# The low part of one weight block in a Strassen-like product: from a VectorE subtraction to a ScalarE negation and an adding DMA

## Chip, core and metric

One core of a Trainium2 chip runs the kernel. The metric is the device time of one execution in microseconds; lower is better. The kernel before took 1702.33 us as the median of three runs (1701.73 to 1704.52).

The engines are named as the profile names them: PE (TensorE matmuls; PEld is its weight load), DVE (VectorE), ACT (ScalarE), POOL (GpSimd) and SP (SyncE, which here issues most DMAs). Each engine executes its own list of instructions in order and waits for others through semaphores.

## What is computed

A two-layer encoder trunk runs over two requests (512 and 256 tokens, 768 together) with a width of 1024. Layer 0 mixes tokens by windowed attention, layer 1 by a gated short convolution; each is followed by an MLP and a gated embedding.

```python
for i in range(DEPTH):
    h = rms_norm(x, norm_mix[i])
    if i % N_MIXERS == 0:
        x = x + window_attention(h, attn_w_qkv[j], attn_w_o[j], attn_sink[j], band_bias, in_window)
    else:
        x = x + short_conv(h, conv_w_in[j], conv_w[j], conv_w_out[j])
    h = rms_norm(x, norm_mlp[i])
    x = x + jnp.square(jax.nn.relu(h @ mlp_w_up[i])) @ mlp_w_down[i]
    gate = jax.nn.sigmoid(rms_norm(x, norm_ple[i]) @ ple_w_gate[i])
    x = x + (p[i] @ ple_w_proj[i]) * gate
return rms_norm(x, final_norm)
```

Everything is float32. The MLP is 1024 to 4096 and back.

## The kernel before

**Split numbers.** A matrix product of float32 values is made from operands split in two: a high part, which ACT writes by copying the value to the type fp32r, and a low part, the value minus the high part, which DVE writes. A product is then high x high, high x low and low x high.

**Seven-product pairs.** Most of the large products (the MLP's up and down projections, the convolution's input projection) take two weight chunks at a time as a 2x2 block matrix, w11, w12, w21, w22, each 128x512, and form the 2x2 block product with seven block products instead of eight. `Weights7` holds one such pair: two raw chunks `wraw` of 128x1024 loaded by SP (r1 and r2), two sums of blocks (`sum`), and the split parts of four groups: "direct" (w11 and w12, tiles `whi` and `wlo`), "s32" (tiles `zhi`, `zlo`), "s14" (`whi`, `wlo` again, there are two buffers), and "w22" (the right half of the second chunk, tiles `vhi`, `vlo`, one buffer each). `high(group)` is the ACT copy, `low(group)` the DVE subtraction, `split` both.

**The order in a pair.** PE runs seven products of 12 matmuls each, in the order w11, s3, s2, w12, s1, w22, s4. In each, the matmuls with high weights come first and those with low weights last. The PSUM tile `a` accumulates: after w11 it is copied by ACT (tile `c` in `up` and `seven`, two tiles `C` in `down`), then s2 is added to the same `a`. So s2 may start only when ACT has made the copy. While one pair is multiplied, ACT and DVE prepare the next one: its sums, its "s32" and "direct" groups. Its "s14" group and "w22" are made at the start of its own pair.

**Who uses it.** `up(u)` makes one pair of hidden chunks, `down(g, h)` one pair of output chunks, `seven` one pair of the convolution's input projection. In each MLP the jobs run as: two plain `up`s, then for each of seven groups an even `up`, two `down`s, and an odd `up`. So after the first even `up` the cycle is down, down, up (odd), up (even). There are 28 seven-product pairs in each MLP and 11 in the convolution, 67 in all. After an `up` ACT still squares the result in two steps (line 941): tile y2 first, then y1.

**What sets the order.** Inside these functions the order in which the code calls the engines is the order on PE, ACT and DVE (`manual_schedule`). SP and POOL are ordered by the scheduler; POOL does almost nothing before, and its queue holds no DMA.

## Time and profile before

| | before |
|---|---|
| median of three runs | 1702.33 us |
| the profiled execution | 1702.36 us |
| its span, first to last instruction | 1700.6 us |
| DVE busy | 1415.1 us, 83% |
| ACT busy | 907.5 us, 53% |
| POOL busy | 1.0 us |
| DMA, mean | 85 GB/s |

The profile is of one execution. A row of a timeline has the start in us, the length in us, the engine, the line, the operation with output tile and inputs, and in brackets the idle time of the engine before it with what ended it. A row of waits has who waited for whom, the total in us, how often, and the longest. A PE that is busy all the time bounds the kernel; idle time of other engines costs only what it makes PE wait.

### The profile page before, as it was taken

To read this page: it belongs to the slowest core of one execution; us is meant where nothing else is said; L and a number is where in the kernel's file an instruction comes from. 1 tells how busy PE (TensorE), PEld (TensorE's weight loads), DVE (VectorE), ACT (ScalarE), POOL (GpSimd) and SP (SyncE) were. 2 spreads that over 40 slices of the span, in tenths; PEclk is the share of its full clock that TensorE was granted. 3 is DMA by queue.
4 is the path that set the end of the run, shared out by engine and by line. 5 is a ranking of instruction groups with operands and counts; after the bars stand their busy time and mean duration, and the time that the engine had idled before them with its cause. 6 is when DMAs were issued, how large, how long until landed. Compare 5 with 4: busy or idle time off the path is not lost.

```text
span 1700.6 us, 24086 instructions
## 1 busy us (share of the span) xinstructions
PE 1653.7 (97%) x9410; PEld 1592.2 (94%) x9410; DVE 1415.1 (83%) x2304; ACT 907.5 (53%) x1451; POOL 1.0 (0%) x12
## 2 busy tenths in 40 slices
PE   8999999989999999999999999999999999999996
PEld 7887788989999999999999999999999999999986
DVE  6588888889999989987888877858999999998776
ACT  6367756754455455544654334545445445554544
POOL 0000000000000000000000000000000000000000
PEclk9999999999999999999999999999999999999998
DMA  8654322211122211221212212211122211222222
GB/s 262 193 135 121 106 81 81 87 50 67 71 76 74 74 70 68 74 99 66 100 60 75 74 63 76 76 61 50 62 75 74 74 67 72 75 74 86 82 76 93
DMA packets 47843, 144.58 MB, mean 85 GB/s; under 512 B 6081, under 2 KB 10689, under 8 KB 47729
## 3 DMA queue, kind: packets, MB, share of 16 engines
q1 hardware_dynamic: 45168, 139.89, 24.2%
q10 hardware_dynamic: 2560, 3.15, 0.7%
q8 instruction: 74, 1.21, 0.3%
q14 instruction: 41, 0.33, 0.1%
HBM read 123.10 MB, written 10.48 MB: 79 GB/s over the span
## 4 chain that ended last, share of the span: by engine, by line
PE 59%; DVE 29%; ACT 8%; issue 3%; DMA 0%; DVEq 0%; ACTq 0%; SPq 0%
PE a L466 17%; PE mm L129 9%; PE mm L138 8%; PE b L466 4%; PE gate L138 4%; PE B L466 3%; PE C L466 3%; DVE t L361 3%; DVE wlo L445 3%; DVE y L938 3%; DVE zlo L445 2%; DVE act L394 1%; PE d L466 1%; ACT y L941 1%; DVE sum L410 1%
## 5 line engine op out<-in xcount | busy, mean ns | idle before, releaser
L434 ACT ACTIVATE whi<-sum 128x1024 fp32r<-128x1024 f32 x67 | 70.5, 1052 | 146.9 <-PE a L466 146.9
L941 ACT ACTIVATE y<-y 128x768 f32<-128x768 f32 x64 | 53.7, 840 | 144.6 <-DVE y L938 144.5
L466 PE MATMUL a<-xs,whi 128*128 128x384 f32 x624 | 123.4, 340 | 4.2 <-ACT whi L434 3.4
L466 PEld LDWEIGHTS a<-xs,whi 128*128 128x128 f32 x624 | 111.2, 189 | 4.9 <-ACT whi L434 3.7
L466 PE MATMUL a<-t,zhi 128*128 128x384 f32 x536 | 109.9, 338 | 3.4 <-ACT c L1054 3.1
L466 PE MATMUL b<-t,zhi 128*128 128x384 f32 x536 | 109.4, 338 | 0.5 <-ACT ln L254 0.5
L466 PE MATMUL a<-t,whi 128*128 128x384 f32 x536 | 108.8, 336 | 0.9 <-ACT d L1547 0.9
L466 PEld LDWEIGHTS a<-t,zhi 128*128 128x128 f32 x536 | 94.9, 188 | 4.3 <-ACT c L1054 3.8
L466 PE MATMUL a<-act,whi 128*128 128x384 f32 x448 | 96.5, 337 | 0.0
L466 PEld LDWEIGHTS b<-t,zhi 128*128 128x128 f32 x536 | 95.4, 189 | 0.9 <-ACT ln L254 0.9
L466 PEld LDWEIGHTS a<-t,whi 128*128 128x128 f32 x536 | 94.8, 188 | 1.2 <-ACT d L1547 1.2
L445 DVE TENSOR_TENSOR wlo<-wraw,whi 128x1024 fp32r<-128x1024 f32 x72 | 87.7, 1217 | 6.8 <-ACT whi L434 6.8
L445 DVE TENSOR_TENSOR wlo<-sum,whi 128x1024 fp32r<-128x1024 f32 x67 | 81.9, 1222 | 10.2 <-ACT whi L434 10.2
L1110 DVE TENSOR_TENSOR x<-x,a 128x384 f32<-128x384 f32 x112 | 60.7, 552 | 33.9 <-PE a L466 33.6
L434 ACT ACTIVATE zhi<-sum 128x1024 fp32r<-128x1024 f32 x67 | 71.0, 1060 | 22.3 <-DVE sum L410 22.2
L138 PE MATMUL mm<-xs_mix,whi 128*128 128x512 f32 (+1 forms) x320 | 82.9, 342 | 0.0
L434 ACT ACTIVATE whi<-wraw 128x1024 fp32r<-128x1024 f32 x72 | 75.7, 1052 | 11.6 <-PE C L466 6.1
L445 DVE TENSOR_TENSOR zlo<-sum,zhi 128x1024 fp32r<-128x1024 f32 x67 | 81.6, 1217 | 0.0
L466 PEld LDWEIGHTS a<-act,whi 128*128 128x128 f32 x448 | 79.9, 188 | 0.0
L355 ACT ACTIVATE t<-y 128x768 fp32r<-128x768 f32 x56 | 47.1, 842 | 41.2 <-DVE y L346 30.7
L83 ACT ACTIVATE whi<-wraw 128x1024 fp32r<-128x1024 f32 (+2 forms) x49 | 50.0, 1019 | 34.4 <-PE mm L129 13.9
L466 PE MATMUL a<-xs,wlo 128*128 128x384 f32 x312 | 67.7, 339 | 0.1
(316 smaller groups left out, 4488.0 us busy)
## 6 DMA issues: line engine op xcount, KB each, us to landing
wraw<-in_up SPq DMA_DIRECT2D x64, 512.0 KB, 3.5
wraw<-in_down SPq DMA_DIRECT2D x64, 512.0 KB, 3.5
wraw<-in_w_in SPq DMA_DIRECT2D x24, 512.0 KB, 3.5
wraw<-in_gate SPq DMA_DIRECT2D x16, 512.0 KB, 3.5
pj<-pjs SPq DMA_DIRECT2D x16, 384.0 KB, 3.3
wraw<-in_w_q SPq DMA_DIRECT2D x8, 512.0 KB, 4.8
wraw<-in_w_out SPq DMA_DIRECT2D x8, 512.0 KB, 3.5
x_in<-in_x SPq DMA_DIRECT2D x8, 384.0 KB, 7.6
```

Source lines behind the costliest of these rows:

```text
L83: first = act.activation(hi, src, AF.Copy)
L129: pe.matmul(t, lhsT=w, rhs=x[:, o:e], start=first and i == 0 and j == 0, stop=last and i == n - 1 and j == 2)
L138: pe.matmul(ps[:, o:e], lhsT=w, rhs=x[:, o:e], start=i == 0 and j == 0, stop=i == n - 1 and j == 2,)
L355: act.activation(t[0][:], (self.q1, self.q2)[i][:], AF.Copy)
L361: dve.tensor_tensor(lo[:], (self.q1, self.q2)[i][:], hi[:].bitcast(F32), ALU.subtract)
L394: dve.tensor_tensor(lo[:], self.q2[:], hi[:].bitcast(F32), ALU.subtract)
L434: act.activation(hi[:], src, AF.Copy)
L445: dve.tensor_tensor(lo[:], src, hi[:].bitcast(F32), ALU.subtract)
L466: pe.matmul(ps, lhsT=a, rhs=b, start=start and i == 0, stop=i == len(terms) - 1, skip_group_check=True)
L938: dve.scalar_tensor_tensor(t[:, o:e], src, 0.0, r[:, o:e], op, ALU.mult)
L941: act.activation(t[:], t[:], AF.Square)
L1110: dve.tensor_tensor(t[:, o : o + H], t[:, o : o + H], f, op)
```

## The change

Only the w22 group changes, in all 67 pairs. `high("w22")` now does three things: ACT copies w22 to `vhi` as before; ACT then writes `vlo` as the copy of `vhi` times -1; and POOL issues a DMA that reads w22 once more from HBM and adds it to `vlo` in SBUF, so that `vlo` ends as w22 minus its high part. DVE no longer touches `vlo`. And the call moves: from behind the copy of `a` (in `up`, `down` and `seven`) to the very start of the pair, ahead of the split of "s14".

```diff
             self.raw = [fetch(src1), fetch(src2)]
+            self.src2 = src2
...
             act.activation(hi[:], src, AF.Copy)
+            if tag == "v":
+                self.due.remove(group)
+                act.activation(lo[:], hi[:].bitcast(F32), AF.Copy, scale=-1.0)
+                nc.gpsimd.dma_start(lo[:], self.src2[:, CH - n :], accum_op=ALU.add)
             self.parts[group] = hi, lo, src
...
             w.low("s32")
+            w.high("w22")
             w.split("s14")
...
-            w.split("w22")
```

The last three pieces stand in `up`, `down` and `seven` alike (`seven` has other calls between them).

ACT's list, before, around an even `up` that follows an odd one (in the profile from 416.50 us): y_4570 and y_4569 are the squares left from the odd `up`, `whi<-sum` is "s14", `c` the copy of `a`.

```order
L941 ACTIVATE y_4570<-y_4570 128x768
L434 ACTIVATE whi<-sum 128x1024
L941 ACTIVATE y_4569<-y_4569 128x768
L381 ACTIVATE act<-y_4569 128x384
L1054 ACTIVATE c<-a 128x384
L385 ACTIVATE act<-y_4570 128x768
L434 ACTIVATE vhi<-wraw 128x512
```

The same place in the changed kernel:

```order
L946 ACTIVATE y_4574<-y_4574 128x768
L435 ACTIVATE vhi<-wraw 128x512
L438 ACTIVATE vlo<-vhi 128x512
L435 ACTIVATE whi<-sum 128x1024
L946 ACTIVATE y_4573<-y_4573 128x768
L381 ACTIVATE act<-y_4573 128x384
L1060 ACTIVATE c<-a 128x384
L385 ACTIVATE act<-y_4574 128x768
```

`vhi` moved from behind the copy `c` to five places ahead of it, and the new `vlo` stands ahead of it too.

ACT's list in the changed kernel at the next job, the first `down` (in the profile before from 432.27 us; before, its rows were y, whi, y, C x2 and then vhi):

```order
L946 ACTIVATE y_4720<-y_4720 128x768
L435 ACTIVATE vhi<-wraw 128x512
L438 ACTIVATE vlo<-vhi 128x512
L435 ACTIVATE whi<-sum 128x1024
L946 ACTIVATE y_4719<-y_4719 128x768
L1110 ACTIVATE C<-a 128x384 x2
L1131 ACTIVATE p<-b 128x384 x2
```

Here too both stand ahead of the copies `C`, which were third in line behind the first square and are now fifth.

At the end of layer 0, ahead of the convolution, the changed list has the first convolution pair's `vhi` and `vlo` between the last block's copies:

```order
L216 ACT_TABLE_LOAD
L326 ACTIVATE q<-x,vec 128x768
L435 ACTIVATE vhi<-wraw 128x512
L309 ACTIVATE xs_8949<-x,vec 128x768
L326 ACTIVATE q<-x,vec 128x768
L438 ACTIVATE vlo<-vhi 128x512
```

Before, no `vhi` stood there; it came behind the pair's copy `c`.

More of the change, by code (lines that the diff above doesn't have):

```diff
@@ L1112, in down @@
             w.low("s32")
+            w.high("w22")
             w.split("s14")
@@ L1119, in down @@
             c = copies("C", a)
-            w.split("w22")
             v.sums32()
@@ L1527, in seven @@
             w.low("s32")
+            w.high("w22")
             late(first or busy)
@@ L1533, in seven @@
             act.activation(c, a, AF.Copy)
-            w.split("w22")
             late(1)
```

## The prediction

> **What bounds the kernel now.** I read the busy shares first, then one stretch of the MLP, then what PE waited for.

> ```profile
> span 1700.6 us, 24086 instructions
> PE 1653.7 (97%) x9410; PEld 1592.2 (94%) x9410; DVE 1415.1 (83%) x2304; ACT 907.5 (53%) x1451; POOL 1.0 (0%) x12
> PE 59%; DVE 29%; ACT 8%; issue 3%; DMA 0%; DVEq 0%; ACTq 0%; SPq 0%
> ```

> PE is busy 97% of the span. The chain of work that ended last passes through DVE for 29%, which tempts one to price DVE work by that share. The stretch of seven-product pairs says otherwise (columns: PE, PEld, DVE, ACT, POOL busy, clock, DMA share, GB/s):

> ```profile
> 400.00:500.00 100.00, 99.75 (x569) 99.11 (x569) 91.46 (x132) 55.15 (x82) 0.00 (x0) 1.00 0.21 74
> ```

> PE is busy 99.75% at full clock there, so faster DVE can give back only what PE loses by waiting for it. The waits of PE's weight loads for the low part of the group "s32", and for the copy of `a`:

> ```profile
> PEld b L466 <- DVE zlo L445: 8.7, 18, 0.8
> PEld a L466 <- ACT c L1054: 3.8, 2, 2.5
> ```

> All that a lighter DVE can win in the pairs is 8.7 us, 0.5%, in 18 places. Counted in the timeline, twelve of them are one per cycle of four MLP jobs, in the first `down` behind an even `up`. The question is what ACT, which gets the work, does in the same place.

> **The change part by part.** Removed from DVE: one subtraction per pair.

> ```profile
> L445 DVE TENSOR_TENSOR vlo<-wraw,vhi 128x512 fp32r<-128x512 f32 x67 | 46.1, 689 | 25.1 <-ACT vhi L434 25.1
> L434 ACT ACTIVATE vhi<-wraw 128x512 fp32r<-128x512 f32 x67 | 41.6, 621 | 0.0
> ```

> That is 46.1 us of DVE time. ACT gains 67 copies of 128x512; the new one has the shape of `vhi`, so I take its 621 ns, 41.6 us in all. Neither sum stands on PE's path by itself. What matters is the place: `vhi` and `vlo` now run ahead of the copy of `a`.

> *What they add ahead of that copy.* ACT's rows of one cycle, an even `up` whose first product starts at 416.12 and the `down` behind it:

> ```profile
> 416.50 0.85 ACT L941 ACTIVATE y<-y 128x768 f32<-128x768 f32 x1 [4.46 <-DVE y L938]
> ...
> 418.20 0.83 ACT L941 ACTIVATE y<-y 128x768 f32<-128x768 f32 x1
> 419.06 0.53 ACT L381 ACTIVATE act<-y 128x384 fp32r<-128x384 f32 x1
> 419.49 0.47 ACT L1054 ACTIVATE c<-a 128x384 f32<-128x384 f32 x1
> 419.90 0.82 ACT L385 ACTIVATE act<-y 128x768 fp32r<-128x768 f32 x1
> 420.63 0.62 ACT L434 ACTIVATE vhi<-wraw 128x512 fp32r<-128x512 f32 x1
> 421.16 0.47 ACT L1061 ACTIVATE p<-b 128x384 f32<-128x384 f32 x1
> ...
> 432.27 0.85 ACT L941 ACTIVATE y<-y 128x768 f32<-128x768 f32 x1 [4.46 <-DVE y L938]
> 433.03 1.04 ACT L434 ACTIVATE whi<-sum 128x1024 fp32r<-128x1024 f32 x1
> 433.98 0.83 ACT L941 ACTIVATE y<-y 128x768 f32<-128x768 f32 x1
> 434.71 0.85 ACT L1105 ACTIVATE C<-a 128x384 f32<-128x384 f32 x2
> ```

> ACT runs without a gap from the first square to the copy. From `vhi` to the next row is 421.16 - 420.63 = 0.53. `vlo` reads `vhi`, so it can't overlap its end as independent rows do: the step from the square at 418.20 to the `act` that reads it is 0.86 for a length of 0.83, so `vhi` takes 0.62 + 0.03. Together 0.65 + 0.53 = **1.18 us** ahead of the copy. PE's rows in the same cycle:

> ```profile
> 418.21 1.55 PE L466 MATMUL b<-t,zhi 128*128 128x384 f32 x8
> 419.60 0.86 PE L466 MATMUL b<-t,zlo 128*128 128x384 f32 x4
> 420.30 1.56 PE L466 MATMUL a<-t,zhi 128*128 128x384 f32 x8
> ...
> 428.01 0.87 PE L466 MATMUL d<-t,vlo 128*128 128x384 f32 x4
> ...
> 432.91 0.86 PE L466 MATMUL b<-t,zhi 128*128 128x384 f32 x4
> 433.89 0.62 PE L466 MATMUL b<-t,zlo 128*128 128x384 f32 x2
> ...
> 435.40 0.85 PE L466 MATMUL a<-t,zhi 128*128 128x384 f32 x4
> ```

> *Even `up`.* The copy ends at 419.49 + 0.47 = 419.96 and s2 starts at 420.30: room 0.34, of which about 0.06 is the signal (below). The copy moves by 1.18, less what its start moves ahead: the square at 416.50 waits for DVE, which comes out of the odd `up` without its `vlo`, 0.60 earlier by the rows that follow (423.30 - 422.70). So 0.58, less 0.28 of room: PE waits **0.3 us**; 0.9 if DVE's lead is lost.

> *The `down` behind it.* Does the lead hold there? DVE's rows:

> ```profile
> 418.33 1.22 DVE L445 TENSOR_TENSOR wlo<-sum,whi 128x1024 fp32r<-128x1024 f32 x1 [0.32 <-ACT whi L434]
> ...
> 420.76 0.96 DVE L394 TENSOR_TENSOR act<-y,act 128x768 fp32r<-128x768 f32 x1 [0.58 <-ACT act L385]
> ...
> 422.70 0.68 DVE L445 TENSOR_TENSOR vlo<-wraw,vhi 128x512 fp32r<-128x512 f32 x1
> 423.30 0.55 DVE L350 SCALAR_TENSOR_TENSOR y<-y,y 128x384 f32<-128x384 f32 x1
> ...
> 432.62 1.22 DVE L445 TENSOR_TENSOR zlo<-sum,zhi 128x1024 fp32r<-128x1024 f32 x1
> ```

> DVE waits for ACT twice ahead of `vlo`. The second wait, for `act`, which ACT makes right behind the copy, ends 0.58 later, as that copy does. Then `vlo` is missing, 0.60. The two cancel: behind 423.30 DVE runs as before, and the square at 432.27 starts as before. Then `C` ends 1.18 later: 434.71 + 0.47 + 1.18 = 436.36, and with 0.06 for the signal s2 starts at 436.42 instead of 435.40. PE's 0.44 us wait for `zlo` (at 433.89) is inside this; whether it shrinks no longer matters, because the copy is later. **+1.02 us per cycle**, the 0.3 of the `up` included, since ACT's times don't depend on it. Bounds: if DVE's lead reaches the square in full, 1.02 - 0.60 = 0.42; if ACT's delay adds to it by as much, 1.62. There are six such cycles in each MLP: 12 x 1.02 = **+12.2 us** (5.0 to 19.4). A `down` or odd `up` behind a `down` has no square ahead of its copy and ACT idles before it, so it pays nothing.

> *The first even `up` of each MLP*, where PE waits for the copy already:

> ```profile
> 359.08 0.47 ACT L1054 ACTIVATE c<-a 128x384 f32<-128x384 f32 x1
> ...
> 359.61 1.66 PE L466 MATMUL a<-t,zhi 128*128 128x384 f32 x8 [0.95 <-ACT c L1054]
> ...
> 375.44 0.84 ACT L1105 ACTIVATE C<-a 128x384 f32<-128x384 f32 x2
> ...
> 376.13 0.87 PE L466 MATMUL a<-t,zhi 128*128 128x384 f32 x4
> ```

> The copy ends at 359.55 and PE starts at 359.61 (the 0.06 used above). Nothing covers the 1.18 here: +1.18. In the `down` behind it ACT's chain is 0.58 later against that new time: its copy ends half way through 0.84, at about 375.91; + 0.58 + 0.06 is 376.55 against 376.13: +0.4. Together 1.6, twice: **+3.2 us** (2.4 to 3.8).

> *The convolution.* Its copy `c` stands ahead of "s14" and ACT idles there, so `vlo` costs nothing on PE's path. The rows that change:

> ```profile
> 882.11 1.02 DVE L310 SCALAR_TENSOR_TENSOR xs<-x,vec,xs 128x768 fp32r<-128x768 f32 x1 [1.06 <-ACT xs L309]
> ...
> 900.55 0.69 DVE L445 TENSOR_TENSOR vlo<-wraw,vhi 128x512 fp32r<-128x512 f32 x1 [3.33 <-ACT vhi L434]
> ...
> 905.42 1.66 PE L466 MATMUL a<-t,whi 128*128 128x384 f32 x8 [0.92 <-ACT d L1547]
> ...
> 1019.03 0.64 PEld L466 LDWEIGHTS b<-t,zlo 128*128 128x128 f32 x4 [0.42 <-DVE zlo L445]
> ```

> In the first pair DVE stood 3.33 us before `vlo` with the norm's steps queued behind it, and those release PE at 905.42; without `vlo` they go some 1.2 earlier, more than the 0.92 that PE waited: about -1.0. Against it, `vhi` now stands ahead of the `xs` at 882.11, for which DVE waited already: +0.5 to +0.6. Three waits like the one at 1019.03 vanish, DVE being 0.6 or more earlier: -1.3. Together **-1.7 us** (-2.5 to 0).

> *The DMA.* It must land before the last four matmuls of w22. In the `down` `vlo` is written at 432.27 + 0.76 + 1.18 + 0.1 = 434.3 (0.76 is the step from the square to the next row); its first use lies 7.0 us behind s2's start, by three products of 2.1, then 0.7 of w22's high weights, so at 443.4: a lead of 9.1 us, in the even `up` some 10, elsewhere 12. What moves 256 KB here:

> ```profile
> wraw<-in_up SPq DMA_DIRECT2D x64, 512.0 KB, 3.5
> pr<-pj SPq DMA_DIRECT2D x8, 256.0 KB, 2.7
> wraw<-in_w_v SPq DMA_DIRECT2D x2, 384.0 KB, 8.4
> ```

> The trace shows no adding DMA and none issued by POOL. By the nearest rows it lands in 2.7 to 8.4 us; it reads its target too, so I take the 512 KB row, 3.5, plus an unknown time of issue. All of it is inside the lead: 0 us. POOL has nothing else in its queue that holds it: its six memsets of `z` wait until the gates are done and stand between the MLP's DMAs and the convolution's. DMA engines are 21% busy in the stretch, and 256 KB more per pair of 1 MB adds a quarter. [...]

> *Sum.* 12.2 + 3.2 - 1.7 = +13.7. The sum is made against the profiled execution, 1702.36 us (span 1700.6, the rest outside it); the median of the runs, 1702.33, is the same. 1702.4 + 13.7 = **1716 us**; own range by the bounds 1707.3 to 1725.6, say 1707 to 1726.

> **Rivals.**

> *DVE's relief wins.* ACT is 53% busy, and if its copies came in time (say, because the square starts a full 0.6 earlier and `vlo` overlaps `vhi`), only the waits for `zlo` would go, and 0.5 (-1.0 + 0.5) at the convolution's start: 1702.4 - 8.7 - 0.5 = 1693. Against it: 1.18 minus 0.60 exceeds the room in every one of the 14 `down`s. Chance 0.11.

> *Cover on both sides.* The copy ends just as late as `zlo` did before: +0.4 a cycle at most, eaten by the convolution: 1701 to 1706, about no change. A change that does nothing would end here too. Chance 0.11.

> *The adding DMA is late.* If issue and landing take over 9.1 us, PE waits in 14 `down`s, over 10 in 14 `up`s too, over 12 in all 67. At 10 us: 14 x 0.9 = 12.6 more, 1729; at 12 us: 14 x 2.9 + 14 x 1.9 = 67 more, 1783. For it: the unknown issue on POOL, and DVE 91% busy beside it. Against: the longest of the landings above is 8.4 us, and 9.1 is left. [...] Chance 0.12.

> **How the numbers follow.** My forecast has 0.66. A run of this kernel can tell 0.2%, 3.4 us, from no change. Slower: 0.66 + 0.12 + a part of the third case = 0.80; same: 0.09; faster: 0.11. The range: the forecast's own (about 0.6 of the 0.66), the no-change case and a late DMA up to 10 us, 1700 to 1730, about 0.8.

> **What would show it.** Right: PE waits for ACT's `C` of about 1 us in 14 `down`s and for `c` of 0.3 in the even `up`s, `zlo` waits gone or hidden, DVE idle longer ahead of `wlo<-sum`. Wrong: the s2 products starting on time (then DVE's lead reached ACT), or matmuls of `vlo` waiting for a DMA.

## The result and the profile after

The changed kernel takes 1719.61 us (median of 6 runs, 1717.58 to 1722.72) against 1702.36 us before (6 runs, 1701.73 to 1704.52): ratio 1.0102, 95% interval 1.0090 to 1.0114. It is 17 us slower. Its profiled execution has a span of 1718.7 us, 18.1 more than before.

The page of the changed kernel: span, busy shares, and the chain of work that ended last.

```profile
span 1718.7 us, 24302 instructions
PE 1661.1 (97%) x9410; PEld 1594.1 (93%) x9410; DVE 1379.8 (80%) x2237; ACT 953.6 (55%) x1518; POOL 60.0 (3%) x79
PE 67%; DVE 18%; ACT 11%; issue 3%; DMA 0%; ACTq 0%; DVEq 0%; SPq 0%
```

DVE is 35 us lighter, as the change intends, and its share of the chain falls from 29% to 18%. The kernel is slower all the same: that share is no measure of what a lighter engine gives back. The stretch of pairs (same columns as before) shows the loss.

```profile
400.00:500.00 100.00, 98.03 (x555) 96.43 (x554) 86.73 (x123) 56.51 (x85) 6.17 (x7) 1.00 0.32 91
```

PE is busy 98.03% instead of 99.75%, still at full clock. The changed kernel's waits of PE's weight loads (in all, times, longest):

```profile
PEld a L471 <- ACT C L1110: 15.6, 14, 1.2
PEld a L471 <- ACT c L1060: 11.8, 14, 3.7
...
PEld b L471 <- DVE zlo L450: 1.8, 7, 0.8
```

Of 18 waits for `zlo` 7 remain, and 8.7 us have become 1.8. In their place stand 14 waits for `C`, one in each first `down`, which did not exist, and 14 for `c`, one in each even `up`, where there were 2. 27.4 us of waiting for ACT's copies replace 3.8. ACT's rows in the changed kernel, same cycle as in the prediction (even `up`, then the `down`):

```profile
418.30 0.85 ACT L946 ACTIVATE y<-y 128x768 f32<-128x768 f32 x1 [4.51 <-DVE y L943]
419.05 0.62 ACT L435 ACTIVATE vhi<-wraw 128x512 fp32r<-128x512 f32 x1
419.70 0.63 ACT L438 ACTIVATE vlo<-vhi 128x512 fp32r<-128x512 f32 x1
420.24 1.04 ACT L435 ACTIVATE whi<-sum 128x1024 fp32r<-128x1024 f32 x1
421.19 0.83 ACT L946 ACTIVATE y<-y 128x768 f32<-128x768 f32 x1
422.05 0.53 ACT L381 ACTIVATE act<-y 128x384 fp32r<-128x384 f32 x1
422.48 0.47 ACT L1060 ACTIVATE c<-a 128x384 f32<-128x384 f32 x1
...
434.78 0.85 ACT L946 ACTIVATE y<-y 128x768 f32<-128x768 f32 x1 [4.46 <-DVE y L943]
435.53 0.61 ACT L435 ACTIVATE vhi<-wraw 128x512 fp32r<-128x512 f32 x1
436.18 0.63 ACT L438 ACTIVATE vlo<-vhi 128x512 fp32r<-128x512 f32 x1
436.72 1.05 ACT L435 ACTIVATE whi<-sum 128x1024 fp32r<-128x1024 f32 x1
437.67 0.82 ACT L946 ACTIVATE y<-y 128x768 f32<-128x768 f32 x1
438.40 0.84 ACT L1110 ACTIVATE C<-a 128x384 f32<-128x384 f32 x2
```

From the first square to the copy `C` ACT works without a gap: 438.40 - 434.78 = 3.62, where it was 434.71 - 432.27 = 2.44 before. The copy is 1.18 later behind the square, the sum of the two new rows. PE's rows there:

```profile
418.53 1.56 PE L471 MATMUL a<-xs,whi 128*128 128x384 f32 x8
...
420.63 1.55 PE L471 MATMUL b<-t,zhi 128*128 128x384 f32 x8
...
423.01 1.67 PE L471 MATMUL a<-t,zhi 128*128 128x384 f32 x8
...
438.92 0.97 PE L471 MATMUL a<-t,zhi 128*128 128x384 f32 x4 [0.86 <-ACT C L1110]
```

Counted from the even `up`'s s3 (420.63; 418.21 before), s2 of the `up` starts at 2.38 instead of 2.09, and s2 of the `down` at 18.29 instead of 17.19. Both s2 blocks are themselves 0.1 longer (1.67 for 1.56, 0.97 for 0.85): their first matmul comes out of a wait. The whole cycle goes from 59.19 to 60.41 us.

DVE's rows in the changed kernel:

```profile
421.32 1.23 DVE L450 TENSOR_TENSOR wlo<-sum,whi 128x1024 fp32r<-128x1024 f32 x1 [0.90 <-ACT whi L435]
...
425.80 0.56 DVE L350 SCALAR_TENSOR_TENSOR y<-y,y 128x384 f32<-128x384 f32 x1
...
437.80 1.23 DVE L450 TENSOR_TENSOR wlo<-sum,whi 128x1024 fp32r<-128x1024 f32 x1 [1.45 <-ACT whi L435]
```

Most of the time that DVE saved it spends waiting for ACT's `whi`: ahead of `wlo<-sum` it idles 42.0 us in all, 10.2 before.

### The profile page after: what moved, and what is told of

The parts are those of the page before. It is cut to its first block, busy times and chain, and to the rows that moved or that the text cites. A ratio compares the mean times of both kernels' runs of the same rounds, so it can differ in the third digit from the quotient of the medians.

```text
span 1718.7 us, 24302 instructions
## 1 busy us (share of the span) xinstructions
PE 1661.1 (97%) x9410; PEld 1594.1 (93%) x9410; DVE 1379.8 (80%) x2237; ACT 953.6 (55%) x1518; POOL 60.0 (3%) x79
## 4 chain that ended last, share of the span: by engine, by line
PE 67%; DVE 18%; ACT 11%; issue 3%; DMA 0%; ACTq 0%; DVEq 0%; SPq 0%
PE a L471 24%; PE mm L129 9%; PE mm L138 8%; PE B L471 3%; PE C L471 3%; PE c L471 3%; PE d L471 3%; PE b L471 3%; PE gate L138 3%; DVE t L361 2%; DVE wlo L450 2%; ACT whi L435 2%; DVE y L943 1%; ACT y L946 1%; DVE zlo L450 1%
## 5 line engine op out<-in xcount | busy, mean ns | idle before, releaser
L471 PE MATMUL a<-t,zhi 128*128 128x384 f32 x536 | 114.8, 348 | 18.8 <-ACT C L1110 11.2
L435 ACT ACTIVATE vhi<-wraw 128x512 fp32r<-128x512 f32 x67 | 41.9, 625 | 114.4 <-PE B L471 87.9
L435 ACT ACTIVATE whi<-wraw 128x1024 fp32r<-128x1024 f32 x72 | 75.8, 1053 | 12.5 <-PE C L471 7.0
## 6 DMA issues: line engine op xcount, KB each, us to landing
wraw<-in_up SPq DMA_DIRECT2D x64, 512.0 KB, 3.5
wraw<-in_down SPq DMA_DIRECT2D x64, 512.0 KB, 3.5
wraw<-in_w_in SPq DMA_DIRECT2D x24, 512.0 KB, 3.9
wraw<-in_gate SPq DMA_DIRECT2D x16, 512.0 KB, 3.5
vlo<-in_up POOLq DMA_DIRECT2D x28, 256.0 KB, 5.1
vlo<-in_down POOLq DMA_DIRECT2D x28, 256.0 KB, 4.6
pj<-pjs SPq DMA_DIRECT2D x16, 384.0 KB, 3.3
wraw<-in_w_q SPq DMA_DIRECT2D x8, 512.0 KB, 4.8
```

The source lines that it names most:

```text
L435: act.activation(hi[:], src, AF.Copy)
L471: pe.matmul(ps, lhsT=a, rhs=b, start=start and i == 0, stop=i == len(terms) - 1, skip_group_check=True)
```

## The experiments

Theory: the *place* costs the time. `vhi` and `vlo` stand ahead of the copy of `a` in ACT's list, and PE waits for that copy. Rivals: the *adding DMA* costs it (late data, or what it takes from other work), or the *extra ACT work* does, wherever it stands. Each figure by stage below is the time between the first s3 matmuls of two pairs in PE's rows of a profiled execution. Stages are compared and not whole spans, since the stretch ahead of the first pair's s3 alone takes 352.6 to 357.4 us in these executions, in no order that the edits explain.

### The change without its DMA

```diff
                 act.activation(lo[:], hi[:].bitcast(F32), AF.Copy, scale=-1.0)
-                nc.gpsimd.dma_start(lo[:], self.src2[:, CH - n :], accum_op=ALU.add)
```

> The changed kernel without the adding DMA: vlo keeps the negated high part, so the low part of w22 lacks w22 itself. Everything else is as in the change. Theory (ScalarE's order costs the time, the DMA is covered): 1718 to 1720 us, the same waits for c and C. Rival (the DMA costs): 1702 to 1712 us, by what the DMA takes from other transfers or from SBUF.

This kernel leaves out the addition of w22, so its `vlo` is only the negated high part; the order of the work is that of the change. 1719.61 us (4 runs), ratio to before 1.0108 (1.0093 to 1.0123): the same as the change. The DMA costs nothing that these runs can tell where the change has put it. That rival is out.

### The same work at the old place

All three calls of `w.high("w22")` go back to where `w.split("w22")` stood, behind the copy of `a`:

```diff
             w.low("s32")
-            w.high("w22")
             w.split("s14")
...
             act.activation(c, a, AF.Copy)
             late(3 if first else 1)
+            w.high("w22")
             late()
```

> The changed kernel with one thing undone: the ScalarE copy, the negation and the adding DMA stand where the split of w22 stood before, behind the copy of a. Theory (the two ScalarE writes are late only because they stand ahead of the copy of a): the waits of PE for c and C behind an up vanish (14 of about 1.2 us and 12 of about 0.46), and since VectorE has 0.6 us less per pair most waits for zlo vanish too: 1693 to 1700 us. The DMA then has a lead of 5.5 to 6 us instead of 9; it landed in 4.0 to 7.6, median 5.0, in the changed kernel, so some matmuls of vlo may wait up to 2 us. Rival (the adding DMA or its traffic costs the time): still 1712 us or more. Rival (the relief of VectorE is worth nothing): about 1702.

1697.52 us (10 runs), ratio 0.9975 (0.9966 to 0.9984). The same instructions, moved behind the copy, make the kernel faster than before: the place it is, not the amount of ACT work. The same window of this kernel, with the same columns:

```profile
400.00:500.00 100.00, 100.00 (x573) 100.00 (x572) 89.81 (x128) 59.09 (x89) 6.15 (x7) 1.00 0.35 93
```

In this window neither `C` nor `zlo` holds PE any more. What the old place costs is lead: one wait for the DMA appears, 0.5 us. And the convolution gains nothing here (see the account of the prediction).

### Only the copy `vhi` early

No negation and no DMA: DVE subtracts at the old place, and `vhi` alone stays at the start of the pair.

```diff
             act.activation(hi[:], src, AF.Copy)
-            if tag == "v":
-                self.due.remove(group)
-                act.activation(lo[:], hi[:].bitcast(F32), AF.Copy, scale=-1.0)
-                nc.gpsimd.dma_start(lo[:], self.src2[:, CH - n :], accum_op=ALU.add)
...
+            w.low("w22")
             late()
```

> The method of before (VectorE subtracts, in its old place) with only the ScalarE copy vhi moved to the start of the pair. No negation, no DMA. Theory: 0.53 us instead of 1.18 stands ahead of the copy of a, without the lead that VectorE had in the change; in the cycle of four MLP jobs s2 of the first down starts 0.4 us later, or up to 0.9 if VectorE, waiting for ScalarE, comes later by the same 0.53; 0.5 to 1 more in each first even up and the down behind it: 12 x (0.4 to 0.9) + 2 x 1 = 1708 to 1715 us. Rival (the DMA or the work moved to ScalarE costs, not the place): 1702 us or less.

1714.57 us (4 runs), ratio 1.0083 (1.0067 to 1.0098). Its weight loads' waits:

```profile
PEld a L467 <- ACT c L1056: 10.7, 14, 3.0
PEld b L467 <- DVE zlo L446: 9.3, 15, 0.8
PEld a L467 <- ACT C L1107: 7.2, 14, 0.5
```

Half of the new ACT work in the wrong place costs 12.5 of the 17 us, because DVE's relief is missing as well: the copies are late and the waits for `zlo` stay (9.3 us).

### `up` alone, and `down` alone

The change in one of the two functions; the other, and the convolution, have `w.high("w22")` behind the copy as in the second experiment.

```diff
 # up alone: in down
-            w.high("w22")
             w.split("s14")
...
             c = copies("C", a)
+            w.high("w22")
...
 # down alone: in up
-            w.high("w22")
             w.split("s14")
...
             late(3 if first else 1)
+            w.high("w22")
```

> The change in up alone; down and the convolution have the same method behind their copies of a, as in e1. Theory: PE waits 0.46 us for c in each even up behind an odd one, as in the change. In the down behind it vhi and vlo no longer stand ahead of C, so C ends at most 0.3 us later than before and VectorE's lateness decides: a wait of up to 0.2 for zlo or C. Cycles: +0 to +0.2 each against before, the first even ups +1.2 each: 1702 to 1707 us. Rival (the place in up is what costs most, the down pays for the late square it is handed): 1712 or more.

> The change in down alone; up and the convolution as in e1. Theory: no wait in the even up. In the first down 1.18 us stand ahead of C, and as ScalarE made act in time in the up, VectorE hands over the square 0.4 to 0.6 us earlier than before: C ends 0.6 to 0.8 us later than before, s2 starts 0.4 to 0.6 later: 12 x 0.4 to 0.6 plus 2 x 0.4, minus nothing elsewhere: 1706 to 1711 us, between e7 and the change. If VectorE's lead does not reach the square: 1714.

`up` alone: 1709.58 us (5 runs), ratio 1.0032 (1.0016 to 1.0048), above what I expected. `down` alone: 1704.30 us (10 runs), ratio 1.0015 (1.0005 to 1.0025), below it. Both expectations missed, and the stages say how:

| us | before | change | `up` alone | `down` alone |
|---|---|---|---|---|
| first even `up`, layer 0 | 17.62 | 19.22 | 21.16 | 17.88 |
| first even `up`, layer 1 | 19.46 | 21.75 | 21.38 | 18.53 |
| the `down` behind it, layer 0 | 15.41 | 15.55 | 14.70 | 16.46 |
| the `down` behind it, layer 1 | 14.85 | 15.23 | 14.67 | 16.41 |
| five cycles, layer 0 | 295.99 | 302.29 | 297.75 | 296.85 |
| five cycles, layer 1 | 295.72 | 301.93 | 296.36 | 296.24 |

In the cycles each half alone costs 0.1 to 0.2 us (for `up` alone in layer 0 without the 1.1 that a late DMA cost in one `down`), both together 1.25. I had shared 1.25 out between them; it isn't a sum. In `up` alone s2 of the `up` is late by 0.3 and costs 0.1 to restart, and then PE's wait for `zlo` in the `down`, about 0.28 before, is gone: one wait has taken the other's place. In `down` alone DVE is relieved twice of `vlo` while ACT is early in the `up`, so the square starts earlier. ACT's rows of that kernel:

```profile
434.29 0.85 ACT L946 ACTIVATE y<-y 128x768 f32<-128x768 f32 x1 [4.56 <-DVE y L943]
...
437.91 0.84 ACT L1110 ACTIVATE C<-a 128x384 f32<-128x384 f32 x2
```

And PE's:

```profile
419.09 1.56 PE L471 MATMUL a<-xs,whi 128*128 128x384 f32 x8
...
438.44 0.97 PE L471 MATMUL a<-t,zhi 128*128 128x384 f32 x4 [0.30 <-ACT C L1110]
```

From the `up`'s first matmul to the square it is 434.29 - 419.09 = 15.20, against 434.78 - 418.53 = 16.25 in the change and 432.27 - 416.12 = 16.15 before. From the square to the copy it is 3.62, as in the change; but it all happens a microsecond earlier, and PE waits 0.30 instead of 0.86. In the change the `up` has made ACT late, DVE waits for ACT's `act`, and its second lead is eaten up before it reaches the square. That is the cancelling on which the prediction's main term rests, now with its counterpart.

`up` alone is dear because of the first even `up` of each MLP, where PE waits for the copy in any case and the clock falls to half (last section). `down` alone pays more in the `down` behind that `up`, 1.05 and 1.56 us, than in all its cycles; why its first even `up` of layer 1 is 0.93 shorter was not shown. Its profiled execution took 1707.54 us, above the median.

### ACT's new work in its idle time

The two ACT rows move to the end of the pair before, ahead of the squares, where ACT waits for DVE or PE (in the convolution, too, a pair earlier, except for its first pair, which keeps the old place):

```diff
             rectified(y2, y2[:], 0, T, ALU.min)
+            if seven:
+                v.high("w22")
             squared(y2)
...
             w.low("s32")
-            w.high("w22")
             w.split("s14")
...
             added(low, 0, d, ALU.subtract)
+            v.high("w22")
```

> The method of the change (negation and adding DMA), but called near the end of the pair before, ahead of the squares, where ScalarE idles over 4 us before its first square; the first pair of the convolution keeps the old place. Theory: nothing stands ahead of the copies of a that did not before, VectorE is 0.6 us lighter per pair: the 18 waits for zlo (8.7 us) and the convolution's late start shrink: 1691 to 1697 us, waits for c and C near 0. Rival (the DMA costs): 1705 to 1719. Rival (ScalarE's load as such costs): above 1702.

1697.63 us (5 runs), ratio 0.9965 (0.9950 to 0.9980), a little above what I expected. The cycles have no stall left; the convolution's stretch is only 1.0 shorter, not 2.1 as in the change. The difference stands in its first pair, which has the old place here: 16.65 us, 15.47 in the change; the other pairs are as in the change. The next kernel has the edit in the MLPs and the change's own place in the convolution; against the kernel just shown:

```diff
             w.low("s32")
+            w.high("w22")
             late(first or busy)
...
             act.activation(c, a, AF.Copy)
-            if first:
-                w.high("w22")
...
             product7(d, w, "w22", xs, False)
-            if v and not last:
-                v.high("w22")
```

> The best parts together: in the MLPs as e4 (negation and adding DMA ahead of the squares, where ScalarE idles), in the convolution as the change (at the pair's start), where the change took 2.1 us less than before and e4 1.0 less. Theory: 1 us below e4: 1695 to 1697 us, no waits of PE for C, none for zlo in the cycles. Rival: no better than e4 or e1, 1697 to 1698, the difference of the stages being noise of a single profile.

1694.85 us (4 runs), ratio 0.9955 (0.9937 to 0.9972): 0.45% faster than the kernel before and about 25 us faster than the change. From the first pair's s3 to the last's it takes 0.9 us less than the kernel just shown; more than that between the two medians is not explained by the edit. ACT's rows of this kernel, one cycle:

```profile
425.28 0.63 ACT L435 ACTIVATE vhi<-wraw 128x512 fp32r<-128x512 f32 x1 [1.53 <-PE d L471]
426.04 0.63 ACT L438 ACTIVATE vlo<-vhi 128x512 fp32r<-128x512 f32 x1
428.39 0.85 ACT L946 ACTIVATE y<-y 128x768 f32<-128x768 f32 x1 [1.72 <-DVE y L943]
...
430.82 0.85 ACT L1112 ACTIVATE C<-a 128x384 f32<-128x384 f32 x2
```

`vhi` and `vlo` lie in the gap, ACT still idles 1.72 behind them, and from the square to `C` it is 2.43 again. Against the second experiment (0.9966 to 0.9984) the intervals overlap, so which of the two placements is better isn't settled; both beat the kernels before and after.

### The idle time, with DVE subtracting

The placement of the last kernel, but `vlo` made by DVE at the old place: no negation and no DMA. Against that kernel:

```diff
             act.activation(hi[:], src, AF.Copy)
-            if tag == "v":
-                self.due.remove(group)
-                act.activation(lo[:], hi[:].bitcast(F32), AF.Copy, scale=-1.0)
-                nc.gpsimd.dma_start(lo[:], self.src2[:, CH - n :], accum_op=ALU.add)
...
             late(3 if first else 1)
+            w.low("w22")
...
             c = copies("C", a)
+            w.low("w22")
```

> In the MLPs the ScalarE copy vhi stands where ScalarE idles, near the end of the pair before; in the convolution at the pair's start; VectorE subtracts in its old place. No negation, no DMA. It shares with e4 that nothing stands ahead of the copies of a, but VectorE keeps its 0.69 us per pair. Theory (in the MLPs the gain of e1 and e4 is VectorE's relief, 12 waits of about 0.46 us for zlo): those waits stay, 1700 to 1703 us. Rival (the gain comes from ScalarE's freer order behind the copies): 1695 to 1699 us.

1701.01 us (10 runs), ratio 0.9988 (0.9979 to 0.9997). Its waits:

```profile
PEld b L467 <- DVE zlo L446: 7.5, 15, 0.8
```

The waits for `zlo` stay as long as DVE subtracts. So the gain of the best kernel is mainly DVE's relief, as the change must have meant it: 1701.0 with DVE's subtraction, 1694.9 without.

## Why the prediction was right, step by step

The forecast was 1716 us, its own range 1707 to 1726; measured were 1719.6. The sum by terms, against the spans (+18.1):

| term | predicted | measured |
|---|---|---|
| twelve cycles | +12.2 | +14.9 |
| first even `up` of each MLP and the jobs behind it | +3.2 | +4.4 |
| convolution and its start | -1.7 | -1.7 |
| adding DMA | 0 | 0 |
| elsewhere | 0 | +0.5 |

**ACT's 1.18 us ahead of the copy.** Right to the last digit: 3.62 against 2.44 from square to copy.

**Even `up`, 0.3.** s2 starts 0.29 later. So DVE's lead of 0.6 does reach the first square: it stands 0.23 ahead of the `up`'s first matmul (418.30 and 418.53), where it stood 0.38 behind it (416.50 and 416.12).

**The `down`, 1.02.** s2 starts 1.10 later and the square stands 0.1 later against the `up`'s start, where I had it unchanged. The cancelling holds: DVE's row behind the missing `vlo` starts 425.80 - 418.53 = 7.27 behind the `up`'s first matmul, 423.30 - 416.12 = 7.18 before; without the lateness of the `up` (`down` alone) the square comes 0.95 earlier than before. The term is under-sized by what I left out, the restart: each of the two waits costs PE some 0.1 beyond its length, so a cycle comes to 1.24 (14.9 / 12), not 1.02.

**The first even `up`, 1.18, and the `down` behind it, 0.4.** Layer 0, PE's rows before:

```profile
355.76 2.19 PE L466 MATMUL b<-t,zhi 128*128 128x384 f32 x8
...
369.10 1.65 PE L466 MATMUL a<-xs,whi 128*128 128x384 f32 x8 [0.82 <-DVE y L1077]
...
374.63 0.62 PE L466 MATMUL b<-t,zlo 128*128 128x384 f32 x2 [0.39 <-DVE zlo L445]
```

And in the changed kernel:

```profile
356.43 2.25 PE L471 MATMUL b<-t,zhi 128*128 128x384 f32 x8
...
361.46 2.93 PE L471 MATMUL a<-t,zhi 128*128 128x384 f32 x8 [2.08 <-ACT c L1060]
...
365.15 1.57 PE L471 MATMUL c<-xs,whi 128*128 128x384 f32 x8
```

From s3 to s2 it is 361.46 - 356.43 = 5.03, where it was 359.61 - 355.76 = 3.85: +1.18, as said. Two things I had not priced come behind. s2 takes 3.69 to the next product instead of 2.20, while PE's clock is at half for a time (last section): +1.49. And the later waits of 0.82 and 0.39 for DVE are gone, PE coming to them later: from that next product to the `down`'s s3 it is 10.50 instead of 11.57, -1.07. Together +1.60 in layer 0. In layer 1, where the stall is longer (3.35 us, 2.16 before), s2 starts 1.18 later too, and the whole is +2.29. The jobs from that `down` to the first cycle take 0.14 and 0.38 more. So ACT's 1.18 came as I said, but "nothing covers it" did not hold, since most of it was covered later in the same job, and the half clock was missing from the term. That it came out as near as 4.4 to 3.2 is partly luck: in the kernel without the DMA, with the same rows on ACT, the clock stayed full at this place of layer 0 (last section).

**The convolution.** The stretch from its first pair to its last goes from 149.67 to 147.53, -2.14 (predicted -2.3: the stall of 0.92 and the three for `zlo`), and the way into it is 0.44 longer (0.5 to 0.6). Its time is no matter of the DMA: without that it is 147.53 too. But the reason that I gave is not the one that the runs show, so here the number came out partly by luck. I put the gain down to DVE being rid of `vlo`. With the work at the old place DVE is rid of it too, and the stretch is 149.88: nothing is gained, and the three pairs that waited for `zlo` still take 15.06 to 15.07 us (14.67 in the change). With `vhi` early and DVE subtracting, in the kernel with only the copy early and in that of the last experiment, it is 147.53 and 147.54: all of it is gained. The first pair at the old place, and in the last experiment:

```profile
900.81 1.23 DVE L450 TENSOR_TENSOR wlo<-sum,whi 128x1024 fp32r<-128x1024 f32 x1 [1.58 <-ACT whi L435]
...
904.21 1.66 PE L471 MATMUL a<-t,whi 128*128 128x384 f32 x8 [1.09 <-ACT d L1552]
```

```profile
901.45 1.23 DVE L446 TENSOR_TENSOR wlo<-sum,whi 128x1024 fp32r<-128x1024 f32 x1 [0.39 <-ACT whi L435]
...
904.86 1.66 PE L467 MATMUL a<-t,whi 128*128 128x384 f32 x8
```

At the old place `whi` stands behind `vhi` and `vlo` in ACT's list; DVE waits 1.58 for it with the norm's step queued behind, and PE 1.09 for what follows from that. With `vhi` early, `whi` stands right behind the copy `c`, and PE doesn't wait. So in the convolution, too, ACT's order decides: there the early place of `vhi` is what wins.

**The rivals.** DVE's relief is real, but wins only where ACT's new work stands elsewhere (1694.9 to 1697.6, near the 1693 of that rival). The DMA was never late in the change. No cover on both sides: the `C` waits are 1.1 each, not 0.4.

## What to carry to other kernels

When work moves to an engine that is half idle, look at where in its list the new rows stand, not at its share: two rows of 0.6 us ahead of a copy that PE waits for turned a gain of 4 to 8 us into a loss of 17. Put them where that engine waits already, read from the idle times in its timeline. And price two such edits together, since a lead or a lateness won at one place may be eaten or covered at the next: here each half cost 0.1 to 0.2 a cycle and both 1.25.

## What the runs showed of the hardware

**Half clock followed a stall of 2.08 us in one kernel and not one of 2.93 us in another: here the stall's length alone did not decide it.** The windows around the first even `up` of layer 0 and of layer 1 in the changed kernel (the clock is the third number from the end):

```profile
360.00:365.00 5.00, 3.54 (x12) 3.54 (x13) 3.41 (x5) 3.69 (x7) 1.01 (x1) 0.66 0.63 160
1165.00:1185.00 20.00, 16.00 (x73) 15.02 (x73) 17.11 (x27) 11.63 (x17) 0.88 (x1) 0.83 0.24 66
```

And before:

```profile
360.00:365.00 5.00, 5.00 (x31) 5.00 (x30) 4.43 (x8) 3.58 (x7) 0.00 (x0) 1.00 0.01 3
1165.00:1185.00 20.00, 17.34 (x89) 16.78 (x88) 18.17 (x27) 12.04 (x18) 0.00 (x0) 0.91 0.15 56
```

A mean clock of 0.66 over 5 us is 2 x 0.34 x 5 = 3.4 us at half speed; in layer 1 the 0.83 and 0.91 over 20 us make 6.8 against 3.6. In layer 0 half clock followed a stall of 2.08 us, and did not follow one of 0.95. With `up` alone the stall there is 2.78, the eight matmuls behind it take 2.93 us, as in the changed kernel at half clock (1.66 before, at full clock), and that job takes 21.16 us in place of 17.62; in layer 1 its mean clock from 1160 to 1190 us is 0.89, 0.94 before. But at the same place of the kernel without the DMA the stall is longer, 2.93 us, and the clock stays full: the eight matmuls behind it take 1.66 us. Its row, and two stretches of 3.41 us with the columns as above:

```profile
360.74 1.66 PE L470 MATMUL a<-t,zhi 128*128 128x384 f32 x8 [2.93 <-ACT c L1059]
...
356.20:359.61 3.41, 1.61 (x9) 1.29 (x8) 2.03 (x5) 2.24 (x4) 0.00 (x0) 1.00 0.05 18
359.61:363.02 3.41, 2.28 (x13) 2.28 (x14) 2.17 (x3) 3.36 (x6) 0.00 (x0) 1.00 0.46 159
```

**Here a short stall was priced better by the wait of the weight load than by PE's idle time.** The s2 blocks above take about 0.1 us longer behind a stall (1.67 for 1.56, 0.97 for 0.85). In the cycle shown PE's own rows have idle times of 0.13 and 0.86 us ahead of s2, and PEld's have 0.45 and 1.18. The cycle of the best kernel, in which no weight load waits, takes 58.82 us; the changed one takes 1.59 more, near the sum of the weight loads' waits.

**The adding DMA.** Tile `vlo` in the changed kernel: POOL's rows (min, median, max in ns), and from issue to landing:

```profile
L439 POOL DMA_DIRECT2D vlo<-in_up x28: 872/875/1011, 360.4 to 1583.0; - x28
L439 POOL DMA_DIRECT2D vlo<-in_down x28: 862/875/892, 376.8 to 1568.3; - x28
...
DMA to landing us min/median/max: 4.0/5.0/7.6
```

POOL is busy 0.875 us for each, and 256 KB land in 4.0 to 7.6 us, longer than the 3.5 that I took from a plain DMA of twice the size. The lead of 9.0 us and more, from the end of the negation to the first weight load of `vlo`, covers it. Behind the copy of `a` the lead is 5.2 to 7.7 us, and single transfers were late: once in the kernel with the old place (0.5 us), twice with `up` alone (2.0 us in all), twice with `down` alone (1.3). POOL is busy 0.86 to 1.01 us for each issue in these three kernels as in the change, where DVE beside it is busy 87% of the stretch from 400 to 500 us; the prediction had weighed a late DMA beside a busy DVE.
